# Hybrid decoder trunk on one core: memory rows' squares behind a weight cast, block scores directly behind values, compression one slot earlier

## The chip, the cores and the metric

The kernel runs on one core of a Trainium2 chip. The metric is device time in microseconds (us) of one execution. Engines are named as the profile names them: PE is TensorE (matmuls), PEld its weight loads, DVE is VectorE, ACT is ScalarE, POOL is GpSimd, SP is SyncE, which here only issues loads and stores.

## The reference

Input x has 256 tokens of width 1024; there are 256 memory tokens of the same width. Layer 0 is RMS norm, one input projection, three groups of attention heads, a SiLU gate on each, one output projection and the residual. Layer 1 has retention heads and the memory heads; a final RMS norm follows. Cut to what the change touches:

```python
def even_layer(x, mem_n, ...):
    h = rms_norm(x, norm_g)
    (nq, nkc, nvc, nks, nvs, nkw, nvw, ng, nz, mq, mk, mv, mz, eq, ez) = _split(h @ w_in, EVEN_SPLITS)
    kc = nsa_compress(rot(nkc), pe_k, w1_k, w2_k)      # 32-token windows, two small layers
    vc = nsa_compress(heads(nvc), pe_v, w1_v, w2_v)
    a_out = nsa_attention(rot(nq), kc, vc, ...)        # A: 8 heads, softmax
    b_out = moba_attention(rot(mq), rot(mk), heads(mv))  # B: 8 heads, causal softmax
    m_out = memory_attention(heads(eq), mem_n, w_mem_kv)  # M: 4 heads
    y = jnp.concatenate([a_out * silu(nz), b_out * silu(mz), m_out * silu(ez)], -1) @ w_out
    return x + y

mem_n = rms_norm(mem, mem_norm_g)   # x * rsqrt(mean(x * x) + eps) * g
```

With 256 tokens, group B has one block, so it is plain causal attention. The squares in the title are those of mem in this last line.

## The kernel before, in words

**Projections.** A weight unit is 128 rows by 1024 columns in f32. SP loads it into one of 6 buffers `raw`. ACT rounds it to fp32r (`whi`, line 166), DVE subtracts to get the rest (`wlo`, line 174). Each product is then three matmuls, high by high, high by low and low by high (lines 245 to 247), into a PSUM bank named `pj` (or s, t, tr). A unit is 12 matmuls of 512 columns, or 24 of 256. There are 4 buffers of `whi` and `wlo`, so ACT casts a few units ahead.

**Attention in couples.** `couple` works on two pairs of heads at a time: scores of both (16 matmuls on 64-row tiles, two side by side, line 116), masked maxima on DVE (line 580, or 584 for the memory heads), exponentials on ACT (593), reciprocal and scaling mostly on DVE with one piece on ACT (549 to 555), transposes on PE (324), copies of these to SBUF as `pt` on ACT (611), and the values (line 116 again, 64-column tiles) into bank `o`. Then the result is gated (652), rounded (655) and split (657). There are four sparse couples (group A), two block couples (B) and one memory couple in layer 0 (M). The values of a sparse couple include those of the compressed keys (`vcr`).

**Order.** The program records its instructions in the order in which generators yield. A projection (`drive(...)`) is the main stage; each of its yields ends a slot, and in each slot every active side task takes one step. `AT` holds slots before which a task does not go on. `take` hands out PSUM banks that are free, in the order of the tags given; while `crowded` is set, bank tr is not handed out. `waiting` holds couples and the results they need. The order so made is fixed: each engine works through its list from the front, and waits there for data from the other engines. SP's loads stand in such a list too.

**The memory group.** `memory_rows` multiplies the transposed memory by its gain. `memory_scale` loads the memory token rows, squares and sums them on ACT (line 418, in `row_scale`), takes the inverse root on DVE (lines 132 to 137) and spreads it over the partitions with a matmul (879, copied by 881 to `rbm`). `memory_keys` projects keys and values of the memory. `tables1` makes the sines for layer 1 (lines 478, 451 to 462), which need another table on ACT than the exponentials.

**Compression.** `compressed` rotates and transposes (739, 740) from slot AT["cmp"] on, sums windows (759), and from AT["hid"] on runs 64 small matmuls (line 116, `tmp` by `v`), an exponential (771) and the second layer (779, 781), whose result is copied to `kcbd` and `vcr` (785, 788).

Of the kernel before, what the change touches and what calls it, by code (L numbers as in the profile page):

```python
# [30 lines left out]
BANKS = {"pj": 3, "tr": 1, "t": 1, "s0": 1, "s1": 1, "o": 1}  # L31
FREE = ("s0", "s1", "t", "tr", "o")
NEG = -1e30
AT = {"rows": 4, "rows1": 4, "spread": 12, "ret": 75, "nsa": 12, "cmp": 15, "blk": 18, "hid": 24}
MAGIC = 12582912.0
PI_LO = 3.1415925
BASE = 16512 + 32 + 416 + 32
# [24 lines left out]
def trunk(  # L62
# [123 lines left out]
    waiting, first, active, made, slot, free = deque(), [], [], set(), [0], {}  # L186
# [16 lines left out]
    def take(n=1, tags=FREE[:4]):  # L203

        while sum(is_free(tag) for tag in tags) < n:
            yield
        got = [tag for tag in tags if is_free(tag)][:n]
        for tag in got:
            free[tag] = 1 << 30
        return got  # L210
# [6 lines left out]
    def drive(stage, every=1):  # L217

        for i, _ in enumerate(stage):
            if i % every == 0:  # L220
                turn()
# [6 lines left out]
    def pause(n):  # L228

        for _ in range(n):  # L230
            yield
# [6 lines left out]
    def making(task, *names):  # L238

        yield from task  # L240
        made.update(names)
# [231 lines left out]
    def tables1():  # L473

        yield from until(AT["ret"])
        rows = load(cs[:, 64:].bitcast(I32), posrow.to_broadcast([P, T]))
        yield from until(AT["ret"] + 4)
        V.tensor_scalar(sn[:, 64:], rows, cpak[:, C_RFREQ : C_RFREQ + 1], None, op0=ALU.mult)
        yield from angles(slice(64, 320))

    def norms():

        yield from until(AT["rows"])
        yield from row_scale(xrow, rstd0, D, AT["rows1"])
        yield from until(AT["spread"])
        tag, = yield from take()
# [67 lines left out]
                else:  # L554
                    V.tensor_scalar(p[:, hh, a], p[:, hh, a], sm[:, hh, tok : tok + 1], None, op0=ALU.mult)  # L555

    def couple(jobs, causal, products, close, name, need=None):

        spans, cols, blocks = (SPAN, 384, range(3)) if causal else (HALF, 512, (0, 2, 1, 3))
        tags = yield from take(4, FREE)  # L560
        ss, todo = [], []
        for i, (q, k, gate) in enumerate(jobs):
            ss.append([bank(tag) for tag in tags[2 * i : 2 * i + 2]])
            for tok, a in enumerate(spans):
                for hh in range(2):
                    rows = slice(64 * hh, 64 * hh + 64)
                    todo.append((ss[i][hh][:, a], q[rows, tok * P : (tok + 1) * P], k[rows, : a.stop - a.start], True, True))
        side_by_side(todo)
        yield
        ps, ms, ns, pts = [[None] * 2 for _ in range(4)]  # L570

        def maxima(i):

            ps[i] = tl("p", [P, 2, 512], 2)
            ms[i] = tl("mx", [P, 2, 2], 4)
            ns[i] = tl("sm", [P, 2, 2], 4)
            for hh in range(2):
                if causal:
                    for tok, a in enumerate(spans):
                        V.tensor_tensor_reduce(ps[i][:, hh, a], ss[i][hh][:, a],  # L580
                                               cpak[:, C_CAUSAL + a.start : C_CAUSAL + a.stop], -1.0, 3e38,
                                               ALU.add, ALU.min, ms[i][:, hh, tok : tok + 1])
                else:
                    V.tensor_reduce(ms[i][:, hh], ss[i][hh].rearrange("p (a k) -> p a k", a=2), AX.X, ALU.max, negate=True)
            if causal:
                give(*tags[2 * i : 2 * i + 2])

        def exponentials(i):

            for hh in range(2):  # L590
                for tok, a in enumerate(spans):
                    src = ps[i][:, hh, a] if causal else ss[i][hh][:, a]
                    S.activation(ps[i][:, hh, a], src, AF.Exp, bias=ms[i][:, hh, tok : tok + 1],  # L593
                                 scale=-1.0 if causal else 1.0, accum_out=ns[i][:, hh, tok : tok + 1])
            if not causal:
                give(*tags[2 * i : 2 * i + 2])

        def scale(i):

            softmax_scale(ps[i], ns[i], spans, jobs[i][2], 0 if jobs[i][2] is None and causal else 3)  # L600

        def turned(i):

            held = yield from take(2, FREE)
            return [(tag, transposes([ps[i][:, hh, b * P : (b + 1) * P] for b in blocks], tag)) for hh, tag in enumerate(held)]

        def copies(i, held):

            pts[i] = tl("pt", [P, 2, 512], 2)
            for hh, (tag, b) in enumerate(held):  # L610
                got = S.copy(pts[i][:, hh, :cols], b)
                give(tag)
            return got

        maxima(0)
        yield
        maxima(1)
        exponentials(0)
        yield
        while need is not None and "gates" not in made:  # L620
            yield
        exponentials(1)
        scale(0)
        yield
        scale(1)
        yield
        first = yield from turned(0)
        yield
        copies(0, first)
        second = yield from turned(1)  # L630
        yield
        got = copies(1, second)
        yield
        while need is not None and need not in made:
            yield
        tag, = yield from take(1, ("o",))
        o = bank(tag)
        side_by_side(products(o, pts), got)
        made.add(name)
        yield  # L640
        yield from close(o)
# [6 lines left out]
    def gated(o, szT, y, kts):  # L648

        n = (kts.stop - kts.start) * T  # L650
        yf = tl("tmp2", [P, 512], 3)[:, :n].rearrange("p (k t) -> p k t", t=T)
        V.tensor_tensor(yf, o[:, :n].rearrange("p (k t) -> p k t", t=T), szT[:, kts], ALU.mult)
        give("o")
        yield
        S.copy(y[:, 0, kts], yf)
        yield
        V.tensor_tensor(y[:, 1, kts], yf, y[:, 0, kts].bitcast(F32), ALU.subtract)
# [18 lines left out]
    def sparse_keys(ps):  # L676
# [4 lines left out]
        def post():  # L681
            yield from until(AT["nsa"])
            rs = []
# [159 lines left out]
    def memory_queries():  # L843
        nonlocal eqT, szm
        ps_e = yield from project_turned((xh, xl))
        eqT = tl("s2", [P, 2, T], NS)
        szm = tl("s2", [P, 2, T], NS)

        def post():
            scaled(ps_e[0], rb0, 0.125, eqT)  # L850
            yield from gate_path(ps_e[1:], rb0, szm)

        active.append(making(post(), "eqT", "szm"))
# [14 lines left out]
    def memory_scale():  # L868
        nonlocal rstdm, rbm
        mrow = [load(tl("raw", [P, 1024], NRAW), memtok[:, tok]) for tok in range(2)]  # L870
        rstdm = tl("rstdm", [P, 2])
        yield
        yield from row_scale(mrow, rstdm, D)
        yield
        rbm = tl("rbm", [P, T])
        tag, = yield from take()
        b = bank(tag)
        for tok in range(2):
            PE.matmul(b[:, tok * P : (tok + 1) * P], rstdm[:, tok : tok + 1].to_broadcast([P, P]), ident, start=True, stop=True)
        yield  # L880
        V.tensor_copy(rbm, b[:, :T])
        give(tag)

    def memory_keys():
        nonlocal memk, memv
        assert {"mh", "rbm"} <= made
        ps = yield from project_mem((mh, ml))
        memk = tl("s2", [P, 2, T], NS)
        memv = tl("s2", [P, 2, T], NS)

        def post():
            mem_keys(ps, rstdm, rbm, memk, memv)
            yield

        active.append(making(post(), "memk"))
# [31 lines left out]
    def block_couple(c):  # L927
        nonlocal yb
        if c == 0:
            yb = tl("y", [P, 2, 4, T], 2, F32R)  # L930

        def products(o, pts):
            todo = []
            for i in range(2):
                todo += causal_products(o[:, i * T : i * T + T], pts[i],
                                        lambda hh, kt: mvt[:, kt, (4 * c + 2 * i + hh) * 64 : (4 * c + 2 * i + hh) * 64 + 64],
                                        True, True)
            return todo

        yield from couple([(mq[:, 2 * c + i], mk[:, 2 * c + i], None) for i in range(2)], True, products,  # L940
                          lambda o: making(gated(o, szb, yb, slice(2 * c, 2 * c + 2)), f"Yb{c}"), f"yb{c}")

    def memory_keys1():
        nonlocal k1, v1m
# [31 lines left out]
    drive(block_values())  # L976
    active.append(making(memory_scale(), "rbm"))
    drive(block_gates())
    waiting.extend(({"mq", "mk", "mvt", "szb", f"yb{c - 1}" if c else "yn3"}, block_couple(c)) for c in range(2))
    drive(memory_queries())  # L980
    crowded = True
    drive(memory_keys())


    def part(acc, tok, c0, n, y, k, wh, wl, start, stop):
# [321 lines left out]
```

## Time and profile before

| | us |
|---|---|
| median of 3 runs | 427.76 (427.15 to 428.31) |
| the profiled execution | 427.74 |
| its span, first to last instruction | 425.9 |
| PE busy | 417.7 |
| DVE busy | 305.7 |
| ACT busy | 245.6 |

The profile shows one execution. A row of its timeline gives start, duration, engine, line, operation, what is written and read, the shape, and in brackets the idle time before it with what ended that. Consecutive instructions of the same line and tiles are merged into one row with their count. Matmuls are pipelined: the duration of one is longer than the distance to the next, so distances between starts are what to read. Times are from the span's start. The granted clock of PE is 0.999 in this execution.

### The profile page before, as it was taken

The numbers are of one execution on the slowest core, as the hardware profiler recorded it, in microseconds if no ns is written. First come the engines' busy times: TensorE is split into PE (matmuls) and PEld (weight loads), VectorE is DVE, ScalarE is ACT, GpSimd is POOL, SyncE is SP. The second block draws the span as 40 slices with busy tenths as digits, with TensorE's granted clock in tenths as the row PEclk, the third lists the DMA queues.
The fourth block names the chain that finished last, engine by engine and source line by source line (L and its number), as shares of the span: only waits on it lengthen the run. The fifth ranks groups of instructions, "written<-read, shape, count | busy, mean of one in ns | idle before, by whom it ended". The sixth has DMA issues, their size and how long they took to land.

```text
span 425.9 us, 7020 instructions
## 1 busy us (share of the span) xinstructions
PE 417.7 (98%) x2620; PEld 361.4 (85%) x2620; DVE 305.7 (72%) x675; ACT 245.6 (58%) x453; POOL 1.9 (0%) x9
## 2 busy tenths in 40 slices
PE   8999999999999999999999999999999999999994
PEld 6889987878889887779999988889998888888884
DVE  3878996977678577588578675677887467685545
ACT  4768476777777586755456344456444445545613
POOL 1000000000000000000000000000000000000000
PEclk9999999999999999999999999999999999999999
DMA  7997545254563852536445545546444555656202
GB/s 247 334 372 254 194 136 192 67 184 160 184 191 110 287 175 97 169 128 195 157 145 168 170 167 168 196 159 198 158 158 159 184 192 175 205 170 189 80 0 99
DMA packets 22801, 74.23 MB, mean 174 GB/s; under 512 B 2928, under 2 KB 4464, under 8 KB 22768
## 3 DMA queue, kind: packets, MB, share of 16 engines
q1 hardware_dynamic: 22192, 73.14, 52.2%
q10 hardware_dynamic: 576, 0.66, 0.6%
q8 instruction: 20, 0.33, 0.3%
q14 instruction: 13, 0.11, 0.1%
HBM read 72.73 MB, written 1.05 MB: 173 GB/s over the span
## 4 chain that ended last, share of the span: by engine, by line
PE 92%; DVE 3%; DMA 3%; ACT 1%; issue 0%; SPq 0%; DVEq 0%; ACTq 0%
PE pj L245 23%; PE pj L247 22%; PE pj L246 22%; PE o L116 3%; PE s L409 2%; PE s L324 2%; PE s L116 2%; PE t L324 1%; DMA raw<-in_w 1%; PE tr L245 1%; PE tr L247 1%; PE tr L246 1%; DMA raw<-in_memtok 1%; PE t L116 1%; PE s L246 1%; PE s L247 1%
## 5 line engine op out<-in xcount | busy, mean ns | idle before, releaser
L174 DVE TENSOR_TENSOR wlo<-raw,whi 128x1024 fp32r<-128x1024 f32 (+1 forms) x118 | 142.1, 1207 | 61.8 <-ACT whi L166 59.7
L166 ACT CAST whi<-raw 128x1024 fp32r<-128x1024 f32 (+1 forms) x118 | 121.7, 1036 | 88.4 <-PE pj L247 38.0
L245 PE MATMUL pj<-whi,big 128*128 128x512 f32 (+2 forms) x256 | 97.3, 383 | 0.0
L246 PE MATMUL pj<-wlo,big 128*128 128x512 f32 (+2 forms) x256 | 96.1, 376 | 0.0
L247 PE MATMUL pj<-whi,big 128*128 128x512 f32 (+2 forms) x256 | 95.8, 374 | 0.0
L245 PE MATMUL pj<-big,whi 128*128 128x256 f32 x256 | 73.6, 287 | 0.0
L247 PE MATMUL pj<-big,wlo 128*128 128x256 f32 x256 | 72.6, 284 | 0.0
L246 PE MATMUL pj<-big,whi 128*128 128x256 f32 x256 | 72.5, 283 | 0.0
L245 PEld LDWEIGHTS pj<-whi,big 128*128 128x128 f32 x256 | 48.2, 188 | 9.3 <-issue 1.5
L247 PEld LDWEIGHTS pj<-whi,big 128*128 128x128 f32 x256 | 48.2, 188 | 8.7
L246 PEld LDWEIGHTS pj<-wlo,big 128*128 128x128 f32 x256 | 48.3, 189 | 8.1 <-DVE wlo L174 0.4
L245 PEld LDWEIGHTS pj<-big,whi 128*128 128x128 f32 x256 | 49.0, 191 | 1.9 <-issue 1.8
L246 PEld LDWEIGHTS pj<-big,whi 128*128 128x128 f32 x256 | 49.0, 192 | 0.1
L247 PEld LDWEIGHTS pj<-big,wlo 128*128 128x128 f32 x256 | 49.0, 191 | 0.0
L593 ACT ACTIVATE p<-p,mx 128x128 f32<-128x128 f32 (+1 forms) x48 | 21.2, 443 | 5.3 <-DVE mx L580 5.3
L245 PE MATMUL pj<-whi,y 128*128 128x512 f32 x42 | 16.9, 407 | 0.0
L247 PE MATMUL pj<-whi,y 128*128 128x512 f32 x42 | 16.4, 390 | 0.0
L246 PE MATMUL pj<-wlo,y 128*128 128x512 f32 x42 | 16.3, 391 | 0.0
L555 DVE TENSOR_SCALAR p<-p,sm 128x256 f32<-128x256 f32 (+1 forms) x48 | 12.7, 322 | 0.6
L343 ACT ACTIVATE big<-raw,vec 128x256 fp32r<-128x256 f32 x16 | 7.7, 505 | 5.2 <-DMA vec<-in_vec 2.5
L553 ACT ACTIVATE p<-p,sm 128x256 f32<-128x256 f32 (+1 forms) x16 | 7.6, 484 | 4.9 <-DVE sm L549 4.0
L580 DVE CUSTOM_DVE_ANT_0 p<-s,cst 128x128 f32<-128x128 f32 (+1 forms) x24 | 7.1, 355 | 4.4 <-PE s L116 4.3
(349 smaller groups left out, 644.5 us busy)
## 6 DMA issues: line engine op xcount, KB each, us to landing
raw<-in_w SPq DMA_DIRECT2D x90, 512.0 KB, 3.9
raw<-in_wout SPq DMA_DIRECT2D x28, 512.0 KB, 4.1
v<-in_xtok SPq DMA_DIRECT2D x4, 512.0 KB, 6.4
raw<-in_w SPq DMA_DIRECT2D x4, 280.0 KB, 5.3
raw<-in_w SPq DMA_DIRECT2D x4, 256.0 KB, 6.2
v<-in_w SPq DMA_DIRECT2D x2, 512.0 KB, 7.5
raw<-in_memT SPq DMA_DIRECT2D x2, 512.0 KB, 4.2
raw<-in_memtok SPq DMA_DIRECT2D x2, 512.0 KB, 4.9
```

The lines of the kernel that those rows point to most:

```text
L116: ins = PE.matmul(out, lhs, rhs, start=start, stop=stop)
L166: S.copy(hi, raw)
L174: V.tensor_tensor(lo, raw, hi.bitcast(F32), ALU.subtract)
L245: PE.matmul(ps, lh, rh, start=start, stop=False, skip_group_check=shared)
L246: PE.matmul(ps, lh, rl, start=False, stop=False, skip_group_check=shared)
L247: return PE.matmul(ps, ll, rh, start=False, stop=stop, skip_group_check=shared)
L324: PE.transpose(b[:, i * P : (i + 1) * P], a, ident)
L343: S.activation(hi[:, kt], raw[:, kt - k0], AF.Copy, scale=g[:, kt : kt + 1])
L409: PE.matmul(ps_k[tok], x[:, kt, tok * P : (tok + 1) * P], w, start=kt == 0 and i == 0, stop=kt == KT - 1 and i == 2)
L553: S.activation(p[:, hh, a], p[:, hh, a], AF.Copy, scale=sm[:, hh, tok : tok + 1])
L555: V.tensor_scalar(p[:, hh, a], p[:, hh, a], sm[:, hh, tok : tok + 1], None, op0=ALU.mult)
L593: S.activation(ps[i][:, hh, a], src, AF.Exp, bias=ms[i][:, hh, tok : tok + 1], scale=-1.0 if causal else 1.0, accum_out=ns[i][:, hh, tok : ...
```

## The change

The diff has five edits. The compression's slots go from 15 to 14 and from 24 to 23. `memory_scale` pauses two slots instead of one between its loads and its squares, and three before it takes a bank to spread the scale. Block couples no longer wait for the gate `szb` before their scores, and the second of them asks for banks in the order tr, s0, s1, t. The flag `crowded` is set after the memory keys instead of before them. No instruction is added or removed.

```diff
--- before.py
+++ after.py
@@ -31,7 +31,7 @@
 BANKS = {"pj": 3, "tr": 1, "t": 1, "s0": 1, "s1": 1, "o": 1}
 FREE = ("s0", "s1", "t", "tr", "o")
 NEG = -1e30
-AT = {"rows": 4, "rows1": 4, "spread": 12, "ret": 75, "nsa": 12, "cmp": 15, "blk": 18, "hid": 24}
+AT = {"rows": 4, "rows1": 4, "spread": 12, "ret": 75, "nsa": 12, "cmp": 14, "blk": 18, "hid": 23}
 MAGIC = 12582912.0
 PI_LO = 3.1415925
 BASE = 16512 + 32 + 416 + 32
@@ -554,10 +554,10 @@
                 else:
                     V.tensor_scalar(p[:, hh, a], p[:, hh, a], sm[:, hh, tok : tok + 1], None, op0=ALU.mult)
 
-    def couple(jobs, causal, products, close, name, need=None):
+    def couple(jobs, causal, products, close, name, need=None, banks=FREE):
 
         spans, cols, blocks = (SPAN, 384, range(3)) if causal else (HALF, 512, (0, 2, 1, 3))
-        tags = yield from take(4, FREE)
+        tags = yield from take(4, banks)
         ss, todo = [], []
         for i, (q, k, gate) in enumerate(jobs):
             ss.append([bank(tag) for tag in tags[2 * i : 2 * i + 2]])
@@ -869,9 +869,9 @@
         nonlocal rstdm, rbm
         mrow = [load(tl("raw", [P, 1024], NRAW), memtok[:, tok]) for tok in range(2)]
         rstdm = tl("rstdm", [P, 2])
-        yield
+        yield from pause(2)
         yield from row_scale(mrow, rstdm, D)
-        yield
+        yield from pause(3)
         rbm = tl("rbm", [P, T])
         tag, = yield from take()
         b = bank(tag)
@@ -938,7 +938,8 @@
             return todo
 
         yield from couple([(mq[:, 2 * c + i], mk[:, 2 * c + i], None) for i in range(2)], True, products,
-                          lambda o: making(gated(o, szb, yb, slice(2 * c, 2 * c + 2)), f"Yb{c}"), f"yb{c}")
+                          lambda o: making(gated(o, szb, yb, slice(2 * c, 2 * c + 2)), f"Yb{c}"), f"yb{c}",
+                          banks=("tr", "s0", "s1", "t") if c else FREE)
 
     def memory_keys1():
         nonlocal k1, v1m
@@ -976,10 +977,10 @@
     drive(block_values())
     active.append(making(memory_scale(), "rbm"))
     drive(block_gates())
-    waiting.extend(({"mq", "mk", "mvt", "szb", f"yb{c - 1}" if c else "yn3"}, block_couple(c)) for c in range(2))
+    waiting.extend(({"mq", "mk", "mvt", f"yb{c - 1}" if c else "yn3"}, block_couple(c)) for c in range(2))
     drive(memory_queries())
+    drive(memory_keys())
     crowded = True
-    drive(memory_keys())
 
 
     def part(acc, tok, c0, n, y, k, wh, wl, start, stop):
```

Since each engine's list is made by the slots, the edits move many rows. Three places follow. On ACT, at the end of the block values' projection (raw_1083 is the last unit of the block gates' projection, raw_1141 the first of the memory queries', `raw_1257` and `raw_1259` are the memory rows, line 655 and 593 belong to the third and fourth sparse couple). Before:

```order
L611 COPY pt_1275<-o_1250 128x384
L418 ACTIVATE raw_1257,ss_1278<-raw_1257 128x1024
L166 CAST whi_1292<-raw_1083 128x1024
L418 ACTIVATE raw_1259,ss_1278<-raw_1259 128x1024
L166 CAST whi_1363<-raw_1141 128x1024
L655 CAST y_82<-tmp_275_1334 128x256
L593 ACTIVATE p_1336,sm_1338<-p_1336,mx_1337 128x128
```

and now:

```order
L611 COPY pt_1275<-o_1250 128x384
L166 CAST whi_1290<-raw_1083 128x1024
L418 ACTIVATE raw_1257,ss_1318<-raw_1257 128x1024
L418 ACTIVATE raw_1259,ss_1318<-raw_1259 128x1024
L166 CAST whi_1355<-raw_1141 128x1024
L655 CAST y_82<-tmp_275_1333 128x256
L593 ACTIVATE p_1335,sm_1337<-p_1335,mx_1336 128x128
```

Both squares stand behind the cast of raw_1083, and directly behind each other. DVE's inverse root of their sums, which stood between the fourth couple's two sets of maxima, now stands behind both.

On PE, the end of the last sparse couple's values (`o`) and what follows them: mq and mk are the tiles v, `whi` is a unit of the memory queries. Before:

```order
L116 MATMUL o_1528<-pt_1506,s_72_265 64x128 x2
L116 MATMUL o_1528<-s_172_852,vcr_94 64x256 x2
L245 MATMUL pj_1470<-big_70,whi_1422 128x256
L246 MATMUL pj_1470<-big_71,whi_1422 128x256
L247 MATMUL pj_1470<-big_70,wlo_1423 128x256
```

and now:

```order
L116 MATMUL o_1524<-pt_1502,s_72_265 64x128 x2
L116 MATMUL o_1524<-s_172_852,vcr_94 64x256 x2
L116 MATMUL s_309_1536<-v_173_859,v_210_1033 128x128
L116 MATMUL s_310_1537<-v_173_859,v_210_1033 128x128
L116 MATMUL s_309_1536<-v_173_859,v_210_1033 128x256
L116 MATMUL s_310_1537<-v_173_859,v_210_1033 128x256
L116 MATMUL t_1538<-v_173_859,v_210_1033 128x128
L116 MATMUL tr_1539<-v_173_859,v_210_1033 128x128
L116 MATMUL t_1538<-v_173_859,v_210_1033 128x256
L116 MATMUL tr_1539<-v_173_859,v_210_1033 128x256
L245 MATMUL pj_1467<-big_70,whi_1419 128x256
```

The first block couple's scores moved up by one half unit of projection, 12 matmuls, to the values. The second block couple's scores moved in the same way, past 24 matmuls, to the values of the first.

On ACT, in layer 0's output projection, between the memory couple's exponentials and its copies. trig are the angles of layer 1, p the memory couple's exponentials, pt the copies that its values read. Before:

```order
L458 ACT_TABLE_LOAD
L458 ACTIVATE trig_226<-trig_225 128x256
L459 ACTIVATE trig_225<-trig_225 128x256
L593 ACT_TABLE_LOAD
L593 ACTIVATE p_2030,sm_2032<-s_391_2002,mx_2031 128x256 x2
L593 ACTIVATE p_2030,sm_2032<-s_392_2003,mx_2031 128x256 x2
L461 ACTIVATE trig_226<-trig_226 128x256
L462 ACTIVATE trig_226<-trig_226 128x256
L166 CAST whi_2061<-raw_1919 128x1024
L593 ACTIVATE p_2044,sm_2046<-t_2004,mx_2045 128x256 x2
L593 ACTIVATE p_2044,sm_2046<-o_2005,mx_2045 128x256 x2
L553 ACTIVATE p_2030<-p_2030,sm_2032 128x256
```

and now:

```order
L553 ACTIVATE p_2010<-p_2010,sm_2012 128x256
L458 ACT_TABLE_LOAD
L458 ACTIVATE trig_226<-trig_225 128x256
L459 ACTIVATE trig_225<-trig_225 128x256
L461 ACTIVATE trig_226<-trig_226 128x256
L462 ACTIVATE trig_226<-trig_226 128x256
L166 CAST whi_2085<-raw_1941 128x1024
L611 COPY pt_2090<-s_404_2067 128x512
L611 COPY pt_2090<-s_405_2072 128x512
L611 COPY pt_2110<-t_2093 128x512
L611 COPY pt_2110<-o_2098 128x512
```

The sines with their table load moved from before the exponentials to between the second scaling and the four copies; the load back to the exponentials' table moved out of this stretch, to line 516 in layer 1.

## Prediction

> **What bounds the kernel now.** I read the engine shares first, then the tensor engine's waits, then the chain of waits around the longest of them.
>
> ```profile
> PE 417.7 (98%) x2620; PEld 361.4 (85%) x2620; DVE 305.7 (72%) x675; ACT 245.6 (58%) x453; POOL 1.9 (0%) x9
> ```
>
> ```profile
> PE s L324 <- DVE p L555: 1.2, 1, 1.2
> ```
>
> TensorE is busy for 98% of the span, and the number of its instructions does not change. A new order can therefore only win what TensorE waits, or what a matmul takes longer because of its neighbour. The list of its waits has two entries: the program's start, and this one (total, times, longest), which is the target. The chain of waits leads back from it; columns are start, length, what.
>
> ```profile
> 102.57 5.06 DMA raw<-in_memtok
> ...
> 109.83 1.23 DVE wlo L174
> ...
> 117.29 1.03 PE s L324 x6
> ...
> 136.27 0.66 PE s L324 x6
> ```
>
> A load of memory rows holds ScalarE (its square, and a weight cast behind it, are shown below); VectorE's subtraction waits for that cast; and the softmax of the last sparse pair comes late. The same six transposes take 1.03 us there and 0.66 us where they do not wait.
>
> The other losses never show as idle, so I looked at start times. A 256-wide product follows its predecessor after 0.12 us (109.03 less 108.91 in term 2), a 512-wide one after twice that, 0.23.
>
> **Term 1, the squares behind the cast.** ScalarE, VectorE and TensorE (start, duration, instruction, idle before); between them the two memory loads, with their median time to landing and when they were issued:
>
> ```profile
> 103.60 0.49 ACT L611 COPY pt<-o 128x384 f32<-128x384 f32 x1
> 107.71 1.06 ACT L418 ACTIVATE raw<-raw 128x1024 f32<-128x1024 f32 x1 [3.62 <-DMA raw<-in_memtok]
> 108.77 1.03 ACT L166 CAST whi<-raw 128x1024 fp32r<-128x1024 f32 x1
> ...
> 112.00 0.40 ACT L593 ACTIVATE p<-p,mx 128x128 f32<-128x128 f32 x1
> ...
> 115.10 0.50 ACT L593 ACTIVATE p<-p,mx 128x256 f32<-128x256 f32 x1
> ```
>
> ```profile
> 109.83 1.23 DVE L174 TENSOR_TENSOR wlo<-raw,whi 128x1024 fp32r<-128x1024 f32 x1 [5.49 <-ACT whi L166]
> 111.31 0.28 DVE L580 CUSTOM_DVE_ANT_0 p<-s,cst 128x128 f32<-128x128 f32 x1
> ```
>
> ```profile
> raw<-in_memtok SPq DMA_DIRECT2D x2, 512.0 KB, 4.9
> ```
>
> ```profile
> L104 SPq DMA_DIRECT2D raw<-in_memtok x2: 327/327/327, 102.6 to 104.4; - x2
> ```
>
> ```profile
> 115.86 0.28 PE L247 MATMUL pj<-big,wlo 128*128 128x256 f32 x1
> ...
> 118.21 0.71 PE L879 MATMUL t<-cst,rstdm 128*128 128x128 f32 x4
> ```
>
> The order now puts the cast first. It can start when the copy ends, at 104.1, since its weight rows were queued before the memory rows. VectorE's subtraction (1.23) is over by 106.4, and the maxima start when their scores exist (the scores' block ends by 108.7, fence below), about 3 us before the old 111.31. ScalarE gains less: the first square still starts at 107.7. The second row block lands at about 109.1 (issued at 104.4; with a median of 4.9 and 5.06 for the first, it took 4.7), so the squares end at 110.2, the next cast at 111.2. The exponentials then start at about 111.5, half a microsecond earlier than now. Eight of them take 3.6 us (112.00 to 115.60), so the one scaling that ScalarE does ends near 115.6. VectorE needed 6.0 us from its first maximum (111.31) until TensorE could start (117.29); the same work, with the inverse root now behind all maxima, starts at 108.2 and is done near 114.5, since it waits a little for the exponentials. TensorE comes 0.12 after its product of 115.86, at 116.0: the wait is gone, with 0.4 us to spare. From 115.86 to 118.21 are 2.35 us; without a wait, 0.12 and 0.66, so 1.57, of which about 0.05 is the change to the following line-879 matmuls. **1.5 us** won; the bounds are 0.9 (landing 1 us later) and 1.57.
>
> **Term 2, scores directly behind values.** The last sparse pair already has its scores directly behind the values; the first block pair does not.
>
> ```profile
> 105.08 0.28 PE L247 MATMUL pj<-big,wlo 128*128 128x256 f32 x1
> 105.29 1.52 PE L116 MATMUL o<-pt,s 128*64 128x256 f32 x16
> ...
> 108.68 0.39 PE L245 MATMUL pj<-big,whi 128*128 128x256 f32 x1
> 108.91 0.28 PE L246 MATMUL pj<-big,whi 128*128 128x256 f32 x1
> 109.03 0.28 PE L247 MATMUL pj<-big,wlo 128*128 128x256 f32 x1
> ...
> 123.58 0.28 PE L247 MATMUL pj<-big,wlo 128*128 128x256 f32 x1
> ...
> 125.90 0.28 PE L246 MATMUL pj<-big,whi 128*128 128x256 f32 x1
> ...
> 127.09 0.28 PE L247 MATMUL pj<-big,wlo 128*128 128x256 f32 x1
> ...
> 129.03 0.28 PE L246 MATMUL pj<-big,whi 128*128 128x256 f32 x1
> ```
>
> Joined: 108.91 less 105.08, 3.83 us. Apart: 2.32 and 1.94, together 4.26, of which two ordinary products more (0.24). One joint saves 4.26 - 0.24 - 3.83 = 0.19 us: entering costs 0.21 instead of 0.12, leaving 0.23 instead of 0.12, and each is paid once less. The new order has two such joints: **0.38 us**.
>
> **Term 3, compression a slot up.** Its last products (lines 779 and 781) now follow the first pair's scores directly, a third joint between two tilings that never meet in this trace: between 0 and 0.19. Against it, the 64 small products now run into projections instead of transposes; half of a leaving cost, 0.05, is my estimate. I take **0.1**. The rest of the compression (its transposes, its sums, the first pair's exponentials, which now stand behind the compression's copies on ScalarE) is hidden under the block keys' projection; if that cover were gone, the transposes of the first pair would wait, at most for the 3.6 us of eight exponentials.
>
> **Term 4, the memory pair and the output projection.** Because everything moves forward, two waits inside busy stretches should go.
>
> ```profile
> 173.90 1.25 PE L324 MATMUL s<-cst,p 128*128 128x128 f32 x8
> 174.91 0.48 PE L245 MATMUL pj<-whi,y 128*128 128x512 f32 x1
> ...
> 183.50 0.50 PE L245 MATMUL pj<-whi,ym 128*128 128x512 f32 x1
> ...
> 184.56 0.40 PE L245 MATMUL pj<-whi,ym 128*128 128x512 f32 x1
> ```
>
> Eight transposes take 1.01 us here; at 0.11 each (0.66 for six) 0.8 to 0.88, so about 0.2 is waited for p. Three 512-wide products take 1.06 us while ym is finished; three ordinary ones are 0.7, so 0.36. In the new order 24 products stand between the memory values and the first use of ym, instead of 6. **0.55 us**.
>
> **Term 5, a new wait.** The sines of layer 1's angles, with their table load, moved on ScalarE from before the memory pair's exponentials to before its four copies into pt, on which the values wait.
>
> ```profile
> 164.99 1.13 PE L116 MATMUL s<-s,s 64*128 64x256 f32 x8
> ```
>
> ```profile
> 164.83 1.34 DVE L455 SCALAR_TENSOR_TENSOR trig<-trig,trig 128x256 f32<-128x256 f32 x3
> ...
> 167.01 1.28 DVE L584 TENSOR_REDUCE mx<-s 128x2 f32<-128x512 f32 x2
> ...
> 170.88 0.88 DVE L555 TENSOR_SCALAR p<-p,sm 128x256 f32<-128x256 f32 x3
> ```
>
> ```profile
> 166.53 0.42 ACT L458 ACTIVATE trig<-trig 128x256 f32<-128x256 f32 x1 [0.43 <-DVE trig L456]
> ...
> 167.40 1.28 ACT L593 ACT_TABLE_LOAD   x1
> 168.70 0.48 ACT L593 ACTIVATE p<-s,mx 128x256 f32<-128x256 f32 x1
> ...
> 170.51 0.43 ACT L461 ACTIVATE trig<-trig 128x256 f32<-128x256 f32 x1
> ...
> 171.29 1.03 ACT L166 CAST whi<-raw 128x1024 fp32r<-128x1024 f32 x1
> ...
> 175.78 1.08 ACT L611 COPY pt<-s 128x512 f32<-128x512 f32 x2
> ```
>
> Count from the start of the memory scores, at 164.99 in this trace. VectorE: 1.15 until the first eight scores exist, four maxima 2.5, three single angle steps 0.9 (a little less than the 1.34 of the three reductions), a subtraction 1.2, the first scaling with its reciprocal 1.0, the angle reductions with their clamp 1.6, then the second reciprocal, over at 8.5. ScalarE: its scaling to 8.9, load 1.3, four passes 1.7, cast 1.0, four copies 2.1: 15.0. TensorE: sixteen scores 1.9, then 48 products of 0.23, 11.0, and sixteen transposes at 0.11, 1.8: 14.7 to 14.8. So the values wait about **0.2 us**, estimated from these rows; bounds 0 and 1.5.
>
> The same load is where a page would decide otherwise. After the load at 167.40 the exponential starts at 168.70, with nothing between. The Trainium skill, page "ScalarE: Activation LUTs", section "What ACT_TABLE_LOAD costs", adds about 1380 ns of drain to a 1283 ns load; by that the wait would be about 1.6 and the sum 1.4 us smaller. The row agrees with the load and shows no drain, so I sum without it.
>
> **Edits at nothing.** The memory scale (line 879, then rbm) is made later, under the memory queries' projection and still ahead of the memory keys that read it; uncovered, its 0.71 us. One weight load now stands behind the compression's four loads in the queue; its unit is cast several units ahead, and uncovered it would cost up to a load's 5 us. The exponentials' table returns before line 516 of layer 1 instead of inside layer 0: the same number of loads, 1.3 us that delay a tanh whose result is only needed after the whole memory pair there. Bank tr takes the place of o for some transposes; a bank is as good as another.
>
> **Sum.** 1.5 + 0.38 + 0.1 + 0.55 - 0.2 = 2.3 us. The profiled execution took 427.74 us with a span of 425.9, beside a median of 427.76 for the runs, so its own time stands for them: 427.74 - 2.3 = **425.4 us**.
>
> **Rivals.** (a) *The wait shrinks but stays.* The slack of 0.4 us hangs on the second memory load, which still goes through the same queue; VectorE also carries the whole inverse root ahead of the subtraction now. Landing 1 us later leaves 0.6 to 1.2 us: 426.0 to 426.6. Against it: nothing new is queued ahead of that load. (b) *The table load costs more than its row*, or the angle steps hold VectorE longer: the values of the memory pair wait 1.5 instead of 0.2, 426.7. For it: this stretch has no slack by the count above; against it the row at 168.70. (c) *Slower.* The place is the same, ScalarE between the second scaling and the four copies: if the second scaling itself comes after the angle work of both engines (reductions 1.6, load 1.3, passes 1.7) and the cast waits for TensorE to release its buffer, the values wait about 4 us. From 2.5 us of wait the gain is eaten; at 4 it is 429.2. For it, the order fixes sines before copies; against it, the count needs 2.3 us that no row shows. (d) *The order does not help at all*, because another chain sets TensorE's arrival: 427.7. Against it: the chain quoted above, and a list of TensorE's waits that holds nothing else inside the program.
>
> **How the numbers follow.** Forecast 0.72, (a) 0.09, (b) 0.09, (c) 0.05, (d) 0.05. 0.3% of this time is 1.28 us, about what a measurement tells from no change, so faster means under 426.46. The forecast and most of (a) lie there: 0.76; (b), (d) and the rest 0.18; (c) 0.06. The range: all terms at their best give 425.0, and the shown runs scatter by half a microsecond, so 424.6; upwards it takes in (a) and (b), 427.0. The forecast's own range is 424.8 to 426.0.
>
> **What would show it.** Right: no TensorE wait at the line-324 transposes after the fourth gate unit; line 418 behind a cast, VectorE idle before line 174 under 1 us there; the memory pair's values entered with a wait under 0.5 us; no slow products at the first use of ym. Wrong: TensorE idle there still over 0.5 us (a), over 1 us before the memory values (b, c), or joints that save nothing: then the tiling change costs the same between two tilings as out and back.

## The result, and the profile after

The changed kernel takes **425.25 us** (median; 425.00 to 425.38), beside 427.76 for the kernel before in the same comparison: a ratio of 0.9938, with a 95% interval of 0.9922 to 0.9955. The profiled execution took 425.0 us with a span of 422.9, against 427.74 and 425.9. The forecast was 425.4.

TensorE's waits in the changed kernel (total, times, longest) have one entry left, the program's start:

```profile
PE t L400 <- POOL kcbd L716: 1.3, 1, 1.3
```

**The squares.** ScalarE from the last copy into pt to the scaling, in the timeline of the changed kernel (start, duration, instruction, idle before):

```profile
103.25 0.52 ACT L611 COPY pt<-o 128x384 f32<-128x384 f32 x1
103.62 1.10 ACT L166 CAST whi<-raw 128x1024 fp32r<-128x1024 f32 x1
106.70 1.06 ACT L418 ACTIVATE raw<-raw 128x1024 f32<-128x1024 f32 x1 [1.97 <-DMA raw<-in_memtok]
108.00 1.06 ACT L418 ACTIVATE raw<-raw 128x1024 f32<-128x1024 f32 x1 [0.15 <-DMA raw<-in_memtok]
...
110.31 0.40 ACT L593 ACTIVATE p<-p,mx 128x128 f32<-128x128 f32 x1
...
113.83 0.49 ACT L553 ACTIVATE p<-p,sm 128x256 f32<-128x256 f32 x1
```

VectorE and TensorE at the same place:

```profile
104.76 1.23 DVE L174 TENSOR_TENSOR wlo<-raw,whi 128x1024 fp32r<-128x1024 f32 x1 [0.61 <-ACT whi L166]
107.94 0.29 DVE L580 CUSTOM_DVE_ANT_0 p<-s,cst 128x128 f32<-128x128 f32 x1 [0.41 <-PE s L116]
```

```profile
115.66 0.28 PE L247 MATMUL pj<-big,wlo 128*128 128x256 f32 x1
115.78 0.82 PE L324 MATMUL s<-cst,p 128*128 128x128 f32 x6
116.36 0.36 PE L245 MATMUL pj<-big,whi 128*128 128x256 f32 x1
116.56 0.28 PE L246 MATMUL pj<-big,whi 128*128 128x256 f32 x1
```

The transposes follow their predecessor after 0.12 us. VectorE's idle time ahead of the subtraction fell from 5.49 to 0.61, and the maxima start as soon as their scores exist. The cast now covers part of ScalarE's wait for the rows, and what is left of that wait (1.97) delays nothing that TensorE waits for. This time the rows also came sooner: 4.0 us to landing, not 4.9; the landing varies between the profiles, as the experiments show.

```profile
raw<-in_memtok SPq DMA_DIRECT2D x2, 512.0 KB, 4.0
```

**The joints.** TensorE from the product before the last sparse pair's values to the second product behind the first block pair's scores, and from the product before the first sparse pair's scores to the second one behind lines 779 and 781:

```profile
52.48 0.39 PE L247 MATMUL pj<-whi,big 128*128 128x512 f32 x1
...
55.46 0.39 PE L246 MATMUL pj<-wlo,big 128*128 128x512 f32 x1
...
121.29 0.28 PE L247 MATMUL pj<-big,wlo 128*128 128x256 f32 x1
...
125.11 0.28 PE L246 MATMUL pj<-big,whi 128*128 128x256 f32 x1
```

125.11 less 121.29 is 3.82 us, the 3.83 of the joint that was there before; apart it was 4.26 with two products of 0.12 more. The second block pair's joint reads alike: 3.40 us (138.12 to 141.52), where the two groups before took 1.88 and 1.95 (from 141.62 and 146.13) with two such products more, 0.19 saved again. The third joint, the first two rows of the fence above, takes 2.98. In the kernel before, the same two groups stood apart:

```profile
52.46 0.39 PE L247 MATMUL pj<-whi,big 128*128 128x512 f32 x1
...
54.62 0.40 PE L246 MATMUL pj<-wlo,big 128*128 128x512 f32 x1
...
55.55 0.39 PE L247 MATMUL pj<-whi,big 128*128 128x512 f32 x1
...
57.02 0.39 PE L246 MATMUL pj<-wlo,big 128*128 128x512 f32 x1
```

2.16 and 1.47, less two ordinary 512-wide products (0.45): 3.18. This joint too saves 0.20 us, although these two tilings never met in the kernel before.

**The memory pair.** ScalarE, then TensorE, of the changed kernel:

```profile
166.97 0.51 ACT L553 ACTIVATE p<-p,sm 128x256 f32<-128x256 f32 x1 [1.13 <-DVE sm L547]
167.50 1.28 ACT L458 ACT_TABLE_LOAD   x1
168.80 0.42 ACT L458 ACTIVATE trig<-trig 128x256 f32<-128x256 f32 x1
...
172.69 0.61 ACT L611 COPY pt<-o 128x512 f32<-128x512 f32 x1
```

```profile
167.47 1.03 PE L324 MATMUL s<-cst,p 128*128 128x128 f32 x8
...
173.12 0.39 PE L247 MATMUL tr<-whi,y 128*128 128x512 f32 x1
173.44 1.95 PE L116 MATMUL o<-pt,s 128*64 128x256 f32 x16
```

The last copy ends at 173.30 (172.69 and 0.61) and the values start in their turn at 173.44, 0.32 us after the product before them, as the blocks at 52.80 and 158.57 also do, which are entered from a 512-wide product without a wait. So there is no wait, and 0.14 us to spare.

### The profile page after: what moved, and what is told of

It reads as the page before. It is cut to its first block, busy times and chain, and to the rows that moved or that the text cites. A ratio compares the mean times of both kernels' runs of the same rounds, so it can differ in the third digit from the quotient of the medians.

```text
span 422.9 us, 7022 instructions
## 1 busy us (share of the span) xinstructions
PE 415.9 (98%) x2620; PEld 361.8 (86%) x2620; DVE 306.0 (72%) x675; ACT 245.8 (58%) x453; POOL 1.9 (0%) x9
## 4 chain that ended last, share of the span: by engine, by line
PE 98%; DVE 1%; ACT 0%; POOL 0%; issue 0%; DVEq 0%; POOLq 0%
PE pj L245 24%; PE pj L247 23%; PE pj L246 23%; PE o L116 4%; PE s L409 3%; PE s L324 2%; PE s L116 2%; PE t L324 2%; PE t L400 1%; PE tr L246 1%; PE tr L247 1%; PE tr L245 1%; PE t L116 1%; PE s L245 1%; PE s L247 1%; PE s L246 1%
## 5 line engine op out<-in xcount | busy, mean ns | idle before, releaser
L116 PE MATMUL o<-pt,s 128*64 128x256 f32 (+1 forms) x96 | 10.0, 350 | 0.0
```

Of the source, the lines that this page charges most:

```text
L116: ins = PE.matmul(out, lhs, rhs, start=start, stop=stop)
```

## The experiments

Runs of one group share their runs of the kernel before; each ratio is to those, and need not be exactly the quotient of the two medians shown.

| kernel | median us (range) | ratio, 95% interval |
|---|---|---|
| before, first group | 428.03 (426.74 to 430.86) | |
| squares alone | 427.93 (427.15 to 429.23) | 0.9995, 0.9983 to 1.0007 |
| scheduling edits alone | 427.27 (425.83 to 428.98) | 0.9975, 0.9955 to 0.9994 |
| compression alone | 427.89 (426.48 to 429.91) | 0.9997, 0.9980 to 1.0014 |
| change without its banks | 425.51 (425.14 to 425.91) | 0.9939, 0.9924 to 0.9954 |
| before, second group | 428.13 (426.67 to 431.70) | |
| change, one copy | 425.37 (424.76 to 426.33) | 0.9934, 0.9909 to 0.9958 |
| change, three copies | 427.43 (425.85 to 429.26) | 0.9974, 0.9948 to 1.0001 |
| change, longer sines | 426.48 (425.98 to 427.55) | 0.9964, 0.9947 to 0.9980 |
| change, merged transposes | 425.62 (425.31 to 426.52) | 0.9942, 0.9920 to 0.9964 |
| before, third group | 428.16 (426.44 to 429.27) | |
| squares and first joint | 426.09 (425.69 to 427.49) | 0.9955, 0.9940 to 0.9971 |
| change, five copies | 429.88 (428.18 to 431.46) | 1.0049, 1.0030 to 1.0069 |

**The squares alone**

```diff
-        yield
+        yield from pause(2)
         yield from row_scale(mrow, rstdm, D)
-        yield
+        yield from pause(3)
```

> The kernel before with one part of the change alone: the two longer pauses in the memory scale, so that the squares of the memory rows stand behind the weight cast; no joint, compression in its old slot. Additive theory (the prediction's sum): only term 1 acts, 1.5 us, so 427.8 - 1.5 = 426.3, the wait at the transposes of line 324 near 116 us is gone and the rest reads as before. Rival, from the order of the instructions: the turns that move put the memory pair six products later, so that its values are followed directly by the first product that reads ym, where before six products of 0.23 us stood between. In the trace of before ym's first half was there 1.5 us after the values' end and its second half 2.2; so TensorE would wait 1.5 and then 0.3 more there, where it now loses 0.4. That gives back 1.4 of the 1.5 us: 427.6, with a new wait of TensorE on ym.

The part with by far the largest term gains nothing by itself. TensorE's longest wait and its products at ym:

```profile
PE pj L245 <- ACT ym L655: 1.4, 1, 1.4
```

```profile
183.63 0.50 PE L245 MATMUL pj<-whi,ym 128*128 128x512 f32 x1 [1.44 <-ACT ym L655]
183.97 0.40 PE L246 MATMUL pj<-wlo,ym 128*128 128x512 f32 x1
184.36 0.50 PE L247 MATMUL pj<-whi,ym 128*128 128x512 f32 x1
```

The wait at line 324 is gone, and a wait of 1.44 us on ym stands in its place, with the third product late as well (0.39 after the second, 0.23 elsewhere). The rival holds: the terms of the prediction are not additive. The two longer pauses also move the memory pair back until its values are followed directly by their own reader; in the changed kernel the scheduling edits make room there.

**The scheduling edits alone**

```diff
-    waiting.extend(({"mq", "mk", "mvt", "szb", f"yb{c - 1}" ...
+    waiting.extend(({"mq", "mk", "mvt", f"yb{c - 1}" ...
-                          ... f"yb{c}")
+                          ... f"yb{c}", banks=("tr", "s0", "s1", "t") if c else FREE)
-    crowded = True
     drive(memory_keys())
+    crowded = True
```

> The kernel before with the three scheduling edits alone (block pairs no longer need szb, the second pair asks for its own banks, crowded set after the memory keys); squares ahead of the cast and compression as before. Additive theory: two joints at 0.19, the memory pair's transposes 0.2, the wait on ym 0.36, no wait at the memory values: 0.9 to 1.0 us, so 426.8; the wait of 1.2 us at line 324 near 116 us stays as it was. Rival (the end is set by the late squares' chain, and what is won behind it is lost again at the next wait on the same chain): 427.5 or more.

The ratio is a gain of 0.25%, 1.1 us, with an interval from 0.3 to 1.9 us; the medians differ by 0.8. That holds the 0.9 to 1.0 of the additive theory, but the median, 427.27, lies between the theory's 426.8 and the rival's 427.5, so this run does not decide between them. And the wait at line 324 did not stay in its profiled execution (426.07 us, among the shortest). TensorE's values of the last sparse pair, ScalarE's first square, and the place of the old wait:

```profile
106.11 1.52 PE L116 MATMUL o<-pt,s 128*64 128x256 f32 x16
...
116.67 0.28 PE L247 MATMUL pj<-big,wlo 128*128 128x256 f32 x1
116.79 1.00 PE L324 MATMUL s<-cst,p 128*128 128x128 f32 x6
```

```profile
107.18 1.06 ACT L418 ACTIVATE raw<-raw 128x1024 f32<-128x1024 f32 x1 [2.40 <-DMA raw<-in_memtok]
```

The six transposes still take longer than where nothing waits, 0.88 us from the first to the product behind them (117.67) against 0.58 in the changed kernel.

**Compression alone**

```diff
-AT = {... "cmp": 15, "blk": 18, "hid": 24}
+AT = {... "cmp": 14, "blk": 18, "hid": 23}
```

> The kernel before with compression a slot up alone (14 and 23 for 15 and 24). Theory: one joint of 0.19 less 0.05 for the small products that now run into projections: 427.6, inside the scatter of the runs; in the trace the products of line 779 start directly behind the first pair's scores and the distance from the first pair's scores to its values shrinks by 0.2 us. Rival (two tilings that meet cost as much as out and back): nothing in the trace either.

No difference that the timing can tell, as expected; in the trace the distance from the first pair's scores to its values shrinks by 0.22 us, from 18.74 (52.77 to 71.51) to 18.52 (54.02 to 72.54). What this run tells lies elsewhere; the same places as above:

```profile
106.32 1.41 PE L116 MATMUL o<-pt,s 128*64 128x256 f32 x14
...
116.89 0.28 PE L247 MATMUL pj<-big,wlo 128*128 128x256 f32 x1
118.85 1.03 PE L324 MATMUL s<-cst,p 128*128 128x128 f32 x6 [1.68 <-DVE p L555]
```

```profile
109.27 1.06 ACT L418 ACTIVATE raw<-raw 128x1024 f32<-128x1024 f32 x1 [4.27 <-DMA raw<-in_memtok]
```

Three programs with the squares ahead of the cast can now be laid side by side. From the start of the sparse values to the first square: 1.07 us (scheduling edits), 2.42 (before: 107.71 less 105.29), 2.95 (compression). From the last product to the transposes: 0.12, 1.43, 1.96. Between the last two, a first square 0.53 us later is a wait 0.53 us longer, and by that line the wait begins at about 1.1, just above the first. So, as far as one execution of each of three programs can show it, the landing of a 512 KB load passed into TensorE's wait one for one, and it varies: the median time to landing was 3.9, 4.9 and 5.3 us in these three profiles.

**The change without its banks**

```diff
-                          ... f"yb{c}", banks=("tr", "s0", "s1", "t") if c else FREE)
+                          ... f"yb{c}")
```

> The changed kernel without the list of banks for the second block pair; everything else of the change is there. The pair then takes s0, s1, t, tr in the usual order. Theory: a bank is as good as another and the order of the instructions is the same, so 425.25 as the changed kernel. Rival: the output projection's fourth accumulator needs bank tr, which is now released by the second half of the pair's maxima instead of the first; if that is late, its first product waits, up to 1 us: 426.2.

As the changed kernel within the scatter, with the same single entry in the list of waits: this line does nothing for the time that these runs can tell.

**One and three copies ahead of the squares**

```diff
-        yield from pause(2)
+        yield from pause(2); [S.copy(mrow[0], mrow[0]) for _ in range(1)]   # 3
```

> The changed kernel with one more pass of ScalarE ahead of the squares: the first block of memory rows is copied onto itself, about 1.0 us (128x1024); the output stays the same. It takes 0.95 us off the slack of the chain squares, cast, exponentials, scaling, transposes of line 324. Theory A (as the trace of the changed kernel reads: the last scaling ends at 114.3, the transposes start at 115.8, slack 1.4 us): no wait, 425.25. Theory B (the slack of the prediction, 0.4 us): TensorE waits about 0.5 us at line 324 in most runs, 425.8, and the runs scatter.

One copy costs nothing that these runs can tell. Its squares and scaling, and the transposes:

```profile
110.05 1.06 ACT L418 ACTIVATE raw<-raw 128x1024 f32<-128x1024 f32 x1
...
116.92 0.49 ACT L553 ACTIVATE p<-p,sm 128x256 f32<-128x256 f32 x1
```

```profile
116.97 0.28 PE L247 MATMUL pj<-big,wlo 128*128 128x256 f32 x1
117.09 0.82 PE L324 MATMUL s<-cst,p 128*128 128x128 f32 x6
```

ScalarE's scaling ends 0.3 us after the transposes started, and still nothing waits: it makes the last of p's four pieces, which only the last two of the six transposes read, the fifth 0.44 us behind the first (four times 0.109). So in the changed kernel's own profile the slack was 1.9 us (scaling over at 114.32, needed at 116.22).

> As the run with one copy, with three of them, 2.85 us ahead of the squares, 2.7 us later at the exponentials since the second memory load is waited for 0.15 us anyway. Theory A (slack 1.4 us): TensorE waits 1.3 us at line 324 and loses 0.2 more on the transposes behind the wait, 426.75; the runs scatter as the kernel before does, since the landing of the first memory load decides the end again. Theory B (slack 0.4 us): wait 2.3, 427.75. Rival (the chain does not set TensorE's arrival there at all): 425.25.

With three copies the chain decides again, and in the profiled execution it costs more than the waits. TensorE's waits, then the shares of four stretches of a microsecond (busy time with instructions for TensorE, its weight loads, VectorE, ScalarE and GpSimd; then granted clock, DMA share, GB/s):

```profile
PE s L324 <- DVE p L555: 0.9, 1, 0.9
PE s L324 <- ACT p L553: 0.6, 1, 0.6
```

```profile
119.00:120.00 1.00, 0.78 (x4) 0.78 (x5) 0.95 (x5) 1.00 (x2) 0.00 (x0) 0.64 0.37 148
120.00:121.00 1.00, 1.00 (x7) 1.00 (x7) 0.93 (x4) 1.00 (x3) 0.00 (x0) 0.50 0.00 0
121.00:122.00 1.00, 1.00 (x6) 1.00 (x6) 1.00 (x2) 1.00 (x3) 0.00 (x0) 0.50 0.00 0
122.00:123.00 1.00, 1.00 (x8) 1.00 (x7) 0.71 (x2) 0.20 (x2) 0.00 (x0) 0.65 0.38 37
```

The waits lose 2.0 us in this execution (429.26 us, the longest of its runs), and behind them TensorE runs at half clock, at 0.213 us for a 256-wide product, which loses another 1.6. The rival, no loss, is out, but neither theory is met: the median is 2.2 us above the changed kernel's, between the 1.5 of theory A and the 2.5 of theory B, and near the 2.0 that the waits lose here. The half clock does not explain the rest in the median: 3.4 us of it lower an execution's mean granted clock by 0.004, and the runs around the median (427.41 to 427.44) have 0.998; only the two longest, 428.84 and 429.26, have 0.995. The scatter came back as expected, 3.4 us from shortest to longest.

**Longer sines**

```diff
-        S.activation(ang, ang, AF.Sin)
+        S.activation(ang, ang, AF.Sin); [S.copy(ang, ang) for _ in range(3 if cols.start else 0)]
```

> The changed kernel with three more passes of ScalarE behind the sines of layer 1's angles (the angle tile, 128x256, copied onto itself; the output stays the same), about 1.25 us ahead of the cast and of the memory pair's four copies. Theory: this stretch has 0.13 us of slack (the last copy ends at 173.31 and the values, in their turn, start at 173.44), so that the values wait 1.1 us and nothing later takes it back: 426.35. Rival: the passes are covered, since ScalarE idles behind the copies or the values wait for something else: 425.25.

426.48 for 426.35: the theory holds. With 0.14 us to spare, the stretch that term 5 spoke of is tighter than that of term 1, with its 1.9. The values now wait for the last copy:

```profile
174.89 1.95 PE L116 MATMUL o<-pt,s 128*64 128x256 f32 x16 [1.17 <-ACT pt L611]
```

**Merged transposes**

```diff
+            yield
             first = yield from turned(0)
-            yield
-            copies(0, first)
             second = yield from turned(1)
             yield
+            copies(0, first)
             got = copies(1, second)
```

(for the second to fourth sparse pair and both block pairs; likewise the two groups of each rotated projection)

> A version built on the price of leaving a group of transposes (in the trace of the changed kernel the first 512-wide products behind one take 0.315 instead of 0.227 us, 256-wide 0.20 instead of 0.12): the two groups of transposes of one pair are made in one slot, the later one of the two, for the second to fourth sparse pair and both block pairs, and likewise the two of the rotated heads of queries and keys. 29 groups are left ahead of products in layer 0 and 1 instead of 36: 7 times 0.085, 0.6 us; all joints stay. Theory: 425.25 - 0.6 = 424.65, if no copy behind the later group comes late for its values (block pair: copies would end near 120.2, values in their turn start at 121.3). Rival (copies or the rotated heads come late and TensorE waits at the values or at the scores of the first sparse pair, up to 1 us at each): 426 or more.

No gain, so the price that I had read was none. One merged group of twelve:

```profile
117.96 0.28 PE L247 MATMUL pj<-big,wlo 128*128 128x256 f32 x1
118.08 0.82 PE L324 MATMUL s<-cst,p 128*128 128x128 f32 x6
...
119.31 0.37 PE L245 MATMUL pj<-big,whi 128*128 128x256 f32 x1
119.51 0.28 PE L246 MATMUL pj<-big,whi 128*128 128x256 f32 x1
```

From 117.96 to 119.51 are 1.55 us: two products at 0.12 and twelve transposes at 0.109. The first product behind a group does take 0.08 us longer, but it also starts 0.08 sooner behind the last transpose than transposes follow each other. In the changed kernel the six from 115.66 to 116.56 read the same, 0.90. What the merging lost is a new wait in the first merged rotation: near 48.9 us its second four transposes start 0.81 us behind the first four, where four take 0.44 otherwise, 0.4 lost. No version that beats the changed kernel came of it.

**The squares and the first joint**

```diff
 (the squares alone, and)
-    waiting.extend(({"mq", "mk", "mvt", "szb", f"yb{c - 1}" ...
+    waiting.extend(({"mq", "mk", "mvt", f"yb{c - 1}" ...
```

> The squares alone (as in the run only_squares) with one edit more: the block pairs no longer need szb, so that the first pair's scores follow the last sparse pair's values directly. By itself this edit is one joint, 0.19 us. It also brings the memory pair forward by twelve products: twelve products of 0.23 us, 2.7 us in all, stand between the memory pair's values and the first use of ym, more than the 2.2 us that ym takes. Theory (the edits are not additive; the squares' gain was lost at ym and needs this room): the wait of 1.4 us on ym is gone, the gain is 1.5 + 0.2 (joint) + 0.4 (ym) + 0.1 to 0.3: 425.4 to 425.7. Rival (sum over single edits as timed: only_squares gained 0.1, the joint 0.19): 427.5.

One name less in a set, priced at 0.19 us by itself (it was not run alone), brings 1.8 us when added to the squares (427.93 to 426.09): the wait on ym is gone from the list. The median stays 0.4 us above the expected bracket; for 0.3 of it there is a row, since the memory pair's transposes still wait a little in this order, where the eight take 1.09 us instead of 0.79:

```profile
172.57 1.33 PE L324 MATMUL s<-cst,p 128*128 128x128 f32 x8
173.66 0.48 PE L245 MATMUL pj<-whi,y 128*128 128x512 f32 x1
```

**Five copies**

> As the run with three copies, with five, 4.75 us ahead of the squares, 1.9 later than with three. In the profile of the run with three copies, TensorE waited twice within 2 us (1.1 and 0.8) and its granted clock then stood at 0.50 for about 3.3 us, with every product there at 0.213 instead of 0.120. Theory A (a long enough wait trips the clock, every time): TensorE waits about 3.0 and then 0.8 us, and the half clock costs some 1.6 us: 425.25 + 3.6 + 1.6 = 430.5, in nearly all runs. Theory B (the wait alone counts, the half clock in that profile was a chance event): 428.9.

Neither theory. Counted as in the expectation, by the distance between starts less the ordinary one, TensorE waited 1.7 and 0.8 us in the profiled execution (428.24 us), more than the 1.1 and 0.8 with three copies, and the granted clock stayed at 1.00 there. (The list of waits counts only idle time: 1.5 and 0.6, against 0.9 and 0.6.) Of its ten runs, six have a mean granted clock of 0.995 or less and took 429.7 to 431.5; the other four, at 0.998 and 0.999, took 428.2 to 429.2. If the lower means stand for the half clock, which only the one trace with three copies shows, it follows such waits often, not always, and what decides is not the length of the wait alone. What decides it stays open.

## Why the prediction was right, point by point

- **Term 1, 1.5 us.** Right in size: the gap ahead of the transposes went from 1.43 to 0.12 and the group from 0.92 to 0.58, 1.6 together. But the sum treated it as free-standing. With none of the scheduling edits it is worth nothing (squares alone), since the wait moves to ym; one of them, the block pairs that no longer wait for `szb`, is enough to bring it through (squares and first joint). The prediction priced room at ym only as a gain of 0.36; its larger worth is that it lets term 1 count.
- **The slack of 0.4 us** behind term 1 was too small: 1.9 in the changed kernel's profile, and 1.2 with the later landing of the one-copy run (scaling over at 117.41, fifth transpose at 117.53, and 1.06 of copy). The step that failed took ScalarE's scaling as the condition of the first transpose; it is that of the fifth, which gives 0.44. Most of the rest of the 1.9 is the sooner landing in this execution, which is luck: the first square started at 106.70, not 107.7, and the scaling ended at 114.32, not 115.6.
- **Term 2, 0.38 us.** As worked out, 0.19 for each joint, both read in the trace.
- **Term 3, 0.1 us.** The joint gave 0.20, the upper bound. Against it, the first projection product behind the 64 small ones takes 0.22 instead of 0.12, where the first transpose there took 0.16 instead of 0.11 before: 0.05, as estimated. 0.15 in all.
- **Term 4, 0.55 us.** Both waits are gone: the eight transposes take 0.79 instead of 1.01, and the first three products on ym 0.68 instead of 1.06, 0.6 together.
- **Term 5, a wait of 0.2 us.** Mis-sized: 0. The count was close to the trace (from the scores' start at 158.57 to the end of the second scaling 8.91 us, 8.9 forecast), but the load, sines, cast and copies then ended at 14.73, where the count had 15.0, and TensorE came at 14.87, where it had 14.7 to 14.8. The bound from a row, not the page's, decided: the Trainium skill's page "ScalarE: Activation LUTs", section "What ACT_TABLE_LOAD costs", adds some 1380 ns of drain, while the sine stands at 168.80, 0.02 after a load of 1.28 us.
- **Edits at nothing.** The banks do nothing that the runs can tell, as said. The memory scale's four products cost no wait.
- **Rivals.** (a) and (d) fell: no wait is left, and the squares alone and the copies show that this chain did set TensorE's arrival. (b) and (c) name the right place, as the longer sines show: with some 1.3 us more on ScalarE the values waited 1.17 us, near the 1.5 of (b).
- **The sum.** 2.3 us forecast. As measured the terms are 1.6, 0.38, 0.15, 0.6 and 0, 2.7 together. The two spans differ by 3.0, the two profiled times by 2.74, the medians by 2.51. So the terms were in all 0.4 too small, and that the median came within 0.15 of the forecast is in part luck.

**What the prediction did not see** is the scatter. With the squares ahead of the cast, runs spread over 2.8 to 5.0 us (before, scheduling edits, compression; 12 to 29 runs each). Behind it they spread less, though not evenly: 0.4 and 0.8 us in the changed kernel and without its banks (five and six runs), 1.2 to 1.8 with one copy, longer sines, merged transposes, and squares with the first joint (7 to 12 runs), 2.1 with the squares alone. The three profiles laid side by side make the landing of the memory rows one likely source, and the change takes that off TensorE's path; so part of its gain depends on which executions of before it is compared with. Another source has nothing to do with the change: in some profiled executions TensorE also waits for early weights near 9 and 28 us, 1.3 us in all with one copy, 1.8 with squares and first joint, and 0 in the two profiles of before and changed kernel. How much of the scatter each makes was not measured.

## What to carry to other kernels

A wait that is taken away is only won if the next meeting of producer and reader on the same chain has room: look there in the new order of instructions before adding up terms, because an edit that is nearly worthless by itself may be what lets the large one through. Where a wait ends with a DMA, take its landing from several executions, as a range; work that can run without that load belongs ahead of what needs it. A first instruction that looks slow is a price only if the distance from before the group to after it is longer too.

## What the runs showed of the hardware that was not expected

In one traced execution a matmul stream that waited in two pieces lost its clock as well. In the run with three copies TensorE was idle for 0.9 and 0.6 us, with four transposes between; the granted clock falls below full speed in the microsecond from 119, is 0.50 in the next two, and is back during the fourth; by the shares quoted above (0.36, 0.50, 0.50 and 0.35 missing) that is 3.4 us at half clock. The Trainium skill's page "TensorE: Matmul & The Clock Gate", in "Part 1: The HAM clock gate (the "warmup" mystery)", has the clock halved after an idle window of about 3.4 us and full again after a busy one of that length, by windows that run freely. The 3.4 us at half clock agree with the page, and free-running windows would fit that only some runs are hit; but there was no idle stretch of that length here: from the last product ahead of the waits to the first behind them it is 2.9 us (116.62 to 119.53), with six transposes inside. What sets off the half clock is therefore not shown.

The kernel before may have been hit too: of its 74 timings in these groups, the five longest, 430.5 to 431.7 us, are those with a mean granted clock of 0.994 or less. Four of them have 0.993 or 0.994, about what one such stretch would give; the longest has 0.944, which one such stretch would not. None of the five has a trace.
